# Joining three attention groups: merged at the end from three tiles, or one by one under a running maximum in one tile

## The chip, the cores and the metric

The kernel runs on one core of a Trainium2 chip. The time is the device time of one execution in microseconds (us). Three runs of the kernel before gave 960.3, 961.85 and 962.55 us, a median of 961.85. The core's engines are named as in the profile: PE (TensorE, matrix products), DVE (VectorE), ACT (ScalarE), POOL (GpSimd) and SP (SyncE, which here only issues transfers). ACT and POOL issue some transfers too. An engine takes its instructions in the order of the program; what one engine needs from another it waits for.

## The reference

One layer of a decoder trunk over 512 tokens of width 1024, in f32: a norm, one wide projection, two token mixers (retention and dilated attention), gates, an output projection, an MLP and a gated embedding. The change touches the attention alone. It has three groups of four heads (window and dilation 128 and 1, 512 and 4, 2048 and 16). Each group gives an output and a log-denominator, and the groups are joined by a softmax over these:

```
for g, (window, dilation) in enumerate(ATT_PATTERNS):
    o_g, lse_g = dilated_window_attention(aq[:, :, g], ak[:, :, g], av[:, :, g], window, dilation)
    ...
wts = jax.nn.softmax(jnp.stack(lses, axis=0), axis=0)
o = jnp.einsum('gbsh,gbshd->bshd', wts.astype(dt), jnp.stack(outs, axis=0))
att_branch = o.reshape(B, S, ATT_W) @ w_att_out
```

With m the maximum of a row of scores and l the sum of its exponentials, a group's weight is exp(m − M) · l over the sum of the same for all groups, M being the largest m.

## The kernel before, in words

**Products.** A product in f32 precision is made of three rounded ones (`mm3`, L257 to L262): each operand is split into a high and a low part. For weights this is `split_unit` (L234): a unit of 128x1024 arrives as `raw`, ACT writes `whi` (L248), DVE writes `wlo` = raw − whi (L249). PE runs through units six products of 128x512 at a time (`whi`, `wlo`, `whi` against the activations). Four `whi` and four `wlo` tiles exist, and units are split two ahead of their use. Some units are sums of weight blocks: POOL's queue adds a second block into `raw` by an accumulating transfer after the split (L226), or DVE adds two raw tiles (L224).

**Small jobs between products.** The attention's own steps are not written in line. `later(lag, fn, key)` (L111) puts a job into a queue with a due time; `tick` (L120), called after every few products, runs up to two due jobs at every second tick; `force(key)` (L130) runs jobs from the front of the queue until that one is done. So lags set where between the big products a transposition, a softmax or an evacuation stands in each engine's order. Behind that, a scheduler may still exchange neighbours on an engine.

**Attention.** For each group, `att_proj` makes q and k; `scores` (L732) runs four blocks r of 128 queries: four heads of scores into one bank `sc`, `softmax` (L657: DVE adds the mask, takes the maximum m, negates it as `nb`; ACT makes four exponentials `se` with their sums l), a transposition on PE into `pe`, its copy `pT`, and `weigh_values` (L768): values times `pT` into a bank `po`, copied into the group's tile `oT` of 128x4x512. Each of the three groups has its own `oT`. m and l of a group stand in `st`; those of group 0 are brought to the strided order of the others by way of DRAM (`to_strided`).

**Merge.** `merge` (L807) runs after the scores of group 2. DVE and ACT make the three groups' weights (16 columns each), PE transposes them in one bank `pc` (L845), ACT copies them out and its queue stores them in DRAM (`c_dram`, L848), and twelve loads of 256 KB on ACT's queue (L855) spread one row each over all partitions into tiles `cb`. For each head and group DVE multiplies a quarter of `oT` by its `cb` (L861) and adds it to group 0's (L863): twelve multiplications and eight additions of 128x512, four loads ahead of the multiplications. They fall into the time in which PE runs the projections `ret_proj` (its `rz`, `ro` and `kd` are on ACT and DVE, L955 and L570 to L575) and the first of the products of seven (`us`) for retention's values. `merged_split` (L878) splits the joined output much later, for the product with w_att_out.

Of the kernel before, what the change touches and what calls it, by code (L numbers as in the profile page):

```python
# [80 lines left out]
class Block:  # L81
# [575 lines left out]
    def softmax(self, sc, w, nh, mask, m, l):  # L657

        nc = self.nc
        s, e = self.tmp("sm"), self.tmp("se")  # L660
        sv = s[:, : nh * w].rearrange("p (h e) -> p h e", h=nh)
        nc.vector.tensor_tensor(sv, sc[:, : nh * w].rearrange("p (h e) -> p h e", h=nh),
                                mask.unsqueeze(1).to_broadcast([P, nh, w]), op=ALU.add)
        nc.vector.tensor_reduce(m, sv, axis=AX.X, op=ALU.max)
        nb = self.small(nh, "nb")
        nc.vector.tensor_scalar(nb, m, -SCALE, None, op0=ALU.mult)
        for h in range(nh):
            c = slice(h * w, (h + 1) * w)
            nc.scalar.activation(e[:, c], s[:, c], AF.Exp, bias=nb[:, h : h + 1], scale=SCALE,
                                 accum_out=l[:, h : h + 1])  # L670
        return e
# [9 lines left out]
    def attention(self):  # L681

        nc = self.nc
        with self.tc.manual_schedule(engines={nc.scalar.engine, nc.vector.engine}):
            qk = self.att_proj(0, 0), self.att_proj(0, 1)
        nc.sync.dma_start(self.mask, self.a["c_mask"])
        self.left = self.token_factors_seven()
        v0 = self.v_proj()
        self.gain_rows(1, NG)
        self.rot_rows(1)  # L690
        stats = [self.scores(0, *qk, v0, 2)]
        qk = [self.att_proj(1, 0)]
        self.later(4, lambda: stats.__setitem__(0, self.to_strided(stats[0])))
        qk.append(self.att_proj(1, 1))
        pT = self.big("pT")
        stats.append(self.scores(1, *qk, None, held=pT))
        v1, v2 = self.values_seven()
        values = self.weigh_values(1, v1, pT)
        for r in range(NT):
            self.force(("pT", 1, r))  # L700
            self.later(6, lambda r=r: values(r), ("att", 1, r))
        qk = self.att_proj(2, 0), self.att_proj(2, 1)
        self.spare = True
        stats.append(self.scores(2, *qk, v2))
        return stats
# [26 lines left out]
    def scores(self, g, qT, kT, v, lag=14, held=None):  # L732
# [3 lines left out]
        pTs = [[] for _ in range(NT)]  # L736

        def block(r):
# [4 lines left out]
            if not wide:  # L743
# [3 lines left out]
                es.append(self.softmax(sc, P, H, self.mask[:, 128 * (g + 1) : 128 * (g + 2)], m, l))  # L747
# [8 lines left out]
            for e in es:  # L756
                out = None if held is None else held[:, r]
                self.later(8, lambda e=e: pTs[r].append(self.transpose4(e, out)), ("pT", g, r))
            if v is not None:
                self.later(15, lambda: values(r), ("att", g, r))  # L760
# [7 lines left out]
    def weigh_values(self, g, v, pTs):  # L768

        nc = self.nc  # L770
        out = self.oT.setdefault(g, [])

        def values(r):
            if not out:
                out.append(self.big("oT"))
            oT = out[0]
# [13 lines left out]
            if g > 0:  # L790
                self.evac(oT[:, :, r * P : (r + 1) * P], pv)
            else:
                ov = oT.rearrange("p h (q a l) -> p h q a l", q=DIL, a=NT)
                self.evac(ov[:, :, :, r], pv.rearrange("p h (l q) -> p h q l", q=DIL))
# [12 lines left out]
    def merge(self, stats):  # L807
        nc = self.nc
        for r in range(NT):
            self.force(("sc", NG - 1, r))  # L810
        t3 = lambda s: self.sm.tile([P, NT, H], F32, tag="sm16", name=self.nm(s))
        M, den = t3("M"), None
        ms = [st[:, :, 0] for st in stats]
        ls = [st[:, :, 1] for st in stats]
        nc.vector.tensor_tensor(M, ms[0], ms[1], op=ALU.max)
        M2 = t3("M")
        nc.vector.tensor_tensor(M2, M, ms[2], op=ALU.max)
        es = []
        for g in range(NG):
            d, e, w = t3("d"), t3("e"), t3("w")  # L820
            nc.vector.tensor_tensor(d, ms[g], M2, op=ALU.subtract)
            nc.scalar.activation(e, d, AF.Exp, scale=SCALE)
            nc.vector.tensor_tensor(w, e, ls[g], op=ALU.mult)
            es.append(e)
            if den is None:
                den = w
            else:
                n = t3("n")
                nc.vector.tensor_tensor(n, den, w, op=ALU.add)
                den = n  # L830
        inv = t3("inv")
        nc.vector.reciprocal(inv, den)
        cs = []
        for g in range(NG):
            c = t3("c")
            nc.vector.tensor_tensor(c, es[g], inv, op=ALU.mult)
            cs.append(c)
        wide = self.const.tile([P, NG * H * NT], F32, name="cw")
        for g in range(NG):
            nc.vector.tensor_copy(wide[:, g * H * NT : (g + 1) * H * NT].rearrange("p (h r) -> p r h", h=H), cs[g])  # L840
        cd = self.dram.tile([NG * H, S], F32, name="c_dram", tag="c_dram")

        def turn():
            ps = self.bank("pc")
            nc.tensor.transpose(ps[: NG * H * NT, :P], wide, self.ident)  # L845
            turned = self.const.tile([P, P], F32, name="ct")[: NG * H * NT]
            nc.scalar.activation(turned, ps[: NG * H * NT, :P], AF.Copy)
            nc.scalar.dma_start(cd.rearrange("a (r l) -> (a r) l", r=DIL), turned)  # L848

        self.later(1, turn)  # L850
        spread = {}

        def load(h, g):
            c = spread[h, g] = self.tmp("cb")
            nc.scalar.dma_start(c, cd[g * H + h : g * H + h + 1].to_broadcast([P, S]))  # L855

        def weigh(h, g):
            if h == 0:
                self.force(("att", g, NT - 1))
            o, c, n = self.oT[g][0][:, h], spread.pop((h, g)), self.oT[0][0][:, h]  # L860
            nc.vector.tensor_tensor(o, o, c, op=ALU.mult)  # L861
            if g:
                nc.vector.tensor_tensor(n, n, o, op=ALU.add)  # L863

        items = [(h, g) for pair in ((0, 1), (2,)) for h in range(H) for g in pair]
        for i, (h, g) in enumerate(items):
            if i == 0:
                for p in items[:4]:
                    self.later(4, lambda p=p: load(*p))

            def step(i=i, h=h, g=g):
                if i + 4 < len(items):
                    load(*items[i + 4])
                weigh(h, g)
            self.later(7 + i, step, ("O", h, g))


    def merged_split(self, O):  # L878
# [5 lines left out]
        def split(h):  # L884
            self.force(("O", h, 2))
# [240 lines left out]
    def mix(self, A):  # L1126
# [14 lines left out]
        O = self.merged_split(self.oT[0][0])  # L1141
# [4 lines left out]
        for h in range(H):  # L1146
            self.force(("O", h, 2))
# [304 lines left out]
    def run(self):  # L1452
# [3 lines left out]
        self.oT = {}  # L1456
        stats = self.attention()
        self.later(21, lambda: self.merge(stats))
# [31 lines left out]
```

## Time and profile before

| what | value |
|---|---|
| median of three runs | 961.85 us |
| the profiled execution: its own time | 959.34 us |
| its span, first to last instruction | 957.6 us |
| busy: PE, DVE, ACT, POOL | 948.6, 730.6, 539.7, 148.5 us |
| transfers | 159.70 MB, mean 167 GB/s |

The profile is that of one execution. A row of a timeline gives the start and the length of one instruction (or of a run of alike ones, x4), then engine, line, operation, what is written and read, and in square brackets how long the engine sat idle before it and what ended that. A matmul row is 0.39 us long but the next starts 0.23 us after it, since products overlap: starts are to be compared, not lengths. The names of tiles lack their numbers there. "ACTq", "SPq" and POOL's transfer rows are issues of transfers.

### The profile page before, as it was taken

Reading aid. Unit: us, or ns where it says so; the run is one execution under the profiler, and the core shown is the slowest. Engines: PE = TensorE matmul, PEld = TensorE weight load, DVE = VectorE, ACT = ScalarE, POOL = GpSimd, SP = SyncE. Lnnn points to the kernel's source line nnn. Section 1 sums busy time; section 2 is a strip of 40 time slices with the busy share of each in tenths; the row PEclk is TensorE's granted clock in tenths of the full one; section 3 lists DMA queues with packets and bytes.
Section 4 is the critical chain, followed back from the end, with each engine's and each line's share of the span. In section 5 each row is a group of like instructions: output and inputs, shape, how many; then the busy total and the mean of one; then the engine's idle time right before and its main releaser. Section 6 shows DMA issues by size and latency. Waiting matters only on the chain.

```text
span 957.6 us, 14335 instructions
## 1 busy us (share of the span) xinstructions
PE 948.6 (99%) x5380; PEld 831.0 (87%) x5380; DVE 730.6 (76%) x1019; ACT 539.7 (56%) x1027; POOL 148.5 (16%) x132
## 2 busy tenths in 40 slices
PE   9999999999998999999999999999999999999998
PEld 7888888888887888999988888988998998998887
DVE  7878977578866948486937879799499579769953
ACT  6556456434464656477714445883484476467651
POOL 0310231022001111223012211211312202112100
PEclk9999999999999999999999999999999999999999
DMA  9851227434247564869748676968959868876911
GB/s 336 279 175 46 90 66 168 160 117 143 89 111 173 155 134 134 150 189 208 237 122 239 150 180 202 215 146 224 193 150 203 196 188 152 226 173 157 289 49 56
DMA packets 89605, 159.70 MB, mean 167 GB/s; under 512 B 7184, under 2 KB 19136, under 8 KB 89536
## 3 DMA queue, kind: packets, MB, share of 16 engines
q1 hardware_dynamic: 65840, 113.64, 35.8%
q0 software_dynamic: 21760, 41.95, 26.8%
q10 hardware_dynamic: 1936, 3.20, 1.1%
q8 instruction: 42, 0.69, 0.3%
q14 instruction: 27, 0.22, 0.1%
HBM read 150.33 MB, written 6.33 MB: 164 GB/s over the span
## 4 chain that ended last, share of the span: by engine, by line
PE 97%; DVE 2%; DMA 1%; issue 0%; ACT 0%; DVEq 0%
PE pg L260 27%; PE pg L261 27%; PE pg L262 27%; PE pa L262 3%; PE pa L260 3%; PE pa L261 3%; PE po L787 1%; PE ph L585 1%; PE sc L746 1%; DMA cb<-c_dram 1%; PE ry L1054 1%; PE pe L676 1%; PE kv L1041 1%; PE sc L752 1%; PE ry L1056 1%; DVE wlo L249 0%
## 5 line engine op out<-in xcount | busy, mean ns | idle before, releaser
L248 ACT ACTIVATE whi<-raw 128x1024 fp32r<-128x1024 f32 (+1 forms) x251 | 259.7, 1039 | 211.2 <-PE pg L262 85.5
L249 DVE TENSOR_TENSOR wlo<-raw,whi 128x1024 fp32r<-128x1024 f32 (+1 forms) x252 | 299.3, 1198 | 96.4 <-ACT whi L248 95.5
L260 PE MATMUL pg<-whi,hh 128*128 128x512 f32 x296 | 118.1, 400 | 0.0
L262 PE MATMUL pg<-whi,hl 128*128 128x512 f32 x296 | 115.6, 390 | 0.0
L261 PE MATMUL pg<-wlo,hh 128*128 128x512 f32 x296 | 115.3, 389 | 0.0
L260 PE MATMUL pg<-f,whi 128*128 128x256 f32 x384 | 108.7, 283 | 0.3 <-DVE r L1296 0.3
L261 PE MATMUL pg<-f,whi 128*128 128x256 f32 x384 | 108.7, 283 | 0.0
L262 PE MATMUL pg<-f,wlo 128*128 128x256 f32 x384 | 108.7, 283 | 0.0
L260 PE MATMUL pg<-whi,f 128*128 128x512 f32 x192 | 75.2, 392 | 0.0
L261 PE MATMUL pg<-wlo,f 128*128 128x512 f32 x192 | 74.8, 389 | 0.0
L262 PE MATMUL pg<-whi,f 128*128 128x512 f32 x192 | 74.7, 389 | 0.0
L260 PEld LDWEIGHTS pg<-f,whi 128*128 128x128 f32 x384 | 73.7, 192 | 0.7 <-ACT r L1298 0.5
L261 PEld LDWEIGHTS pg<-f,whi 128*128 128x128 f32 x384 | 73.7, 192 | 0.2
L262 PEld LDWEIGHTS pg<-f,wlo 128*128 128x128 f32 x384 | 73.7, 192 | 0.0
L262 PEld LDWEIGHTS pg<-whi,hl 128*128 128x128 f32 x296 | 55.6, 188 | 11.9
L261 PEld LDWEIGHTS pg<-wlo,hh 128*128 128x128 f32 x296 | 55.7, 188 | 10.8
L260 PEld LDWEIGHTS pg<-whi,hh 128*128 128x128 f32 x296 | 55.6, 188 | 10.9 <-ACT whi L248 0.3
L226 POOL DMA_DIRECT2D raw<-in_w_in x24 | 29.3, 1219 | 167.4 <-DVE wlo L249 152.5
L640 POOL TENSOR_TENSOR r<-v,mhalf 128x4 f32<-128x4 f32 x24 | 30.1, 1258 | 147.7 <-DVE v L639 142.0
L226 POOL DMA_DIRECT2D raw<-in_w_down x24 | 29.1, 1216 | 139.9 <-DVE wlo L249 108.8
L226 POOL DMA_DIRECT2D raw<-in_w_up x24 | 29.0, 1210 | 134.8 <-DVE wlo L249 124.4
L224 DVE TENSOR_TENSOR raw<-raw,raw 128x1024 f32<-128x1024 f32 x32 | 38.9, 1219 | 5.3 <-issue 2.9
(276 smaller groups left out, 2257.1 us busy)
## 6 DMA issues: line engine op xcount, KB each, us to landing
raw<-in_w_in SPq DMA_DIRECT2D x72, 512.0 KB, 3.8
raw<-in_w_up SPq DMA_DIRECT2D x32, 512.0 KB, 4.6
raw<-in_w_down SPq DMA_DIRECT2D x32, 512.0 KB, 4.5
raw<-in_w_in POOLq DMA_DIRECT2D x24, 512.0 KB, 6.8
raw<-in_w_up POOLq DMA_DIRECT2D x24, 512.0 KB, 7.3
raw<-in_w_down POOLq DMA_DIRECT2D x24, 512.0 KB, 6.5
x<-in_x SPq DMA_DIRECT2D x8, 512.0 KB, 8.3
raw<-in_w_ret_out SPq DMA_DIRECT2D x8, 512.0 KB, 4.1
```

Source lines behind the costliest of these rows:

```text
L224: self.nc.vector.tensor_tensor(total, total, part, op=ALU.add)
L226: self.nc.gpsimd.dma_start(raw, self.chained[i].rearrange("(k p) n -> p k n", p=P), accum_op=ALU.add)
L248: self.pin(nc.scalar.activation(R(hi[:, i]), raw[:, i], AF.Copy))
L249: nc.vector.tensor_tensor(R(lo[:, i]), raw[:, i], hi[:, i], op=ALU.subtract)
L260: t.matmul(ps, sh, mh, start=first, stop=False, skip_group_check=more)
L261: t.matmul(ps, sh, ml, start=False, stop=False, skip_group_check=more)
L262: t.matmul(ps, sl, mh, start=False, stop=last, skip_group_check=more)
L585: self.nc.tensor.transpose(ps[:, t * P : (t + 1) * P], rots[t][:, h * HD : (h + 1) * HD], self.ident)
L640: nc.gpsimd.tensor_tensor(r, v, self.mhalf[:, :H], op=ALU.pow)
L676: self.nc.tensor.transpose(ps[:, k * P : (k + 1) * P], e[:, k * P : (k + 1) * P], self.ident)
L746: nc.tensor.matmul(sc[:, h * P : (h + 1) * P], qT[:, h, rs], kT[:, h, rs], start=True, stop=True)
L752: nc.tensor.matmul(sc[:, h * 256 : (h + 1) * 256], qT[:, 2 * hp + h, rs], kT[:, 2 * hp + h, (r - 1) * P : (r + 1) * P], start=True, stop=True)
```

## The change

The three groups are joined one after another. Group 1's softmax takes, for each block, the larger of its own maximum and that of group 0 (`past`), group 2's that of the two before. When the scores of group 1 are done, `rescale(1, ...)` makes f = exp(m past − m new) for 16 columns, adds the sums up (l = l new + f · l past), and spreads f over the partitions by way of DRAM as `merge` did; four multiplications scale what group 0 has left in the one tile `oT`. Group 1's weighed values are then added from their bank `po` to that tile instead of being copied to a tile of their own. After the scores of group 2 the same is done once more, and here 1/l is multiplied into f, and into the 16 exponentials' tiles of group 2 (ACT, 128x128 each) before they are transposed. `merge` is gone. Group 2's transpositions are due three ticks later, its values too, and each `force`s its `rescale` first.

```diff
@@ softmax @@
-    def softmax(self, sc, w, nh, mask, m, l):
+    def softmax(self, sc, w, nh, mask, m, l, past=None):
...
         nc.vector.tensor_reduce(m, sv, axis=AX.X, op=ALU.max)
+        if past is not None:
+            nc.vector.tensor_tensor(m, m, past, op=ALU.max)
         nb = self.small(nh, "nb")
@@ attention @@
-        stats = [self.scores(0, *qk, v0, 2)]
+        first = self.scores(0, *qk, None, v0, 2)
         qk = [self.att_proj(1, 0)]
-        self.later(4, lambda: stats.__setitem__(0, self.to_strided(stats[0])))
+        strided = self.to_strided(first)
         qk.append(self.att_proj(1, 1))
         pT = self.big("pT")
-        stats.append(self.scores(1, *qk, None, held=pT))
+        past = self.scores(1, *qk, strided, held=pT)
+        self.later(22, lambda: self.rescale(1, strided, past), ("past", 1))
...
-            self.later(6, lambda r=r: values(r), ("att", 1, r))
+            self.later(8, lambda r=r: values(r), ("att", 1, r))
         qk = self.att_proj(2, 0), self.att_proj(2, 1)
         self.spare = True
-        stats.append(self.scores(2, *qk, v2))
-        return stats
+        last = self.scores(2, *qk, past, v2)
+        self.later(21, lambda: self.rescale(2, past, last), ("past", 2))
@@ scores @@
-                self.later(8, lambda e=e: pTs[r].append(self.transpose4(e, out)), ("pT", g, r))
+                self.later(8 if g < 2 else 11, lambda e=e: turn(e, r, out), ("pT", g, r))
             if v is not None:
-                self.later(15, lambda: values(r), ("att", g, r))
+                self.later(15 if g < 2 else 18, lambda: values(r), ("att", g, r))
+
+        def turn(e, r, out):
+            if g == 2:
+                self.force(("past", 2))
+            pTs[r].append(self.transpose4(e, out))
@@ weigh_values @@
         def values(r):
-            if not out:
-                out.append(self.big("oT"))
-            oT = out[0]
+            if g:
+                self.force(("scaled", g))
+            if not self.oT:
+                self.oT.append(self.big("oT"))
+            oT = self.oT[0]
...
             if g > 0:
-                self.evac(oT[:, :, r * P : (r + 1) * P], pv)
+                rs = oT[:, :, r * P : (r + 1) * P]
+                nc.vector.tensor_tensor(rs, rs, pv, op=ALU.add)
@@ merge, replaced by rescale @@
-    def merge(self, stats):
...
+    def rescale(self, g, past, st):
+
         nc = self.nc
         for r in range(NT):
-            self.force(("sc", NG - 1, r))
+            self.force(("sc", g, r))
         t3 = lambda s: self.sm.tile([P, NT, H], F32, tag="sm16", name=self.nm(s))
...
+        f, l = t3("f"), st[:, :, 1]
+        nc.vector.tensor_tensor(f, past[:, :, 0], st[:, :, 0], op=ALU.subtract)
+        nc.scalar.activation(f, f, AF.Exp, scale=SCALE)
+        w = t3("w")
+        nc.vector.tensor_tensor(w, f, past[:, :, 1], op=ALU.mult)
+        nc.vector.tensor_tensor(l, l, w, op=ALU.add)
+        if g == NG - 1:
+            inv = t3("inv")
+            nc.vector.reciprocal(inv, l)
+            nc.vector.tensor_tensor(f, f, inv, op=ALU.mult)
+            for r in range(NT):
+                e = self.es[g, r]
+                for h in range(H):
+                    c = slice(h * P, (h + 1) * P)
+                    nc.scalar.activation(e[:, c], e[:, c], AF.Copy, scale=inv[:, r, h : h + 1])
+        wide = self.const.tile([P, H * NT], F32, name=f"wide{g}")
+        nc.vector.tensor_copy(wide.rearrange("p (h r) -> p r h", h=H), f)
+        d = self.dram.tile([H, S], F32, name=f"f_dram{g}", tag=f"f_dram{g}")
+        spread = []
 
         def turn():
             ps = self.bank("pc")
-            nc.tensor.transpose(ps[: NG * H * NT, :P], wide, self.ident)
...
+            nc.tensor.transpose(ps[: H * NT, :P], wide, self.ident)
+            turned = self.const.tile([P, P], F32, name=f"turned{g}")[: H * NT]
+            nc.scalar.activation(turned, ps[: H * NT, :P], AF.Copy)
+            nc.scalar.dma_start(d.rearrange("a (r l) -> (a r) l", r=DIL), turned)
+
+        def load():
+            spread.append(self.big("fb"))
+            for h in range(H):
+                nc.scalar.dma_start(spread[0][:, h], d[h : h + 1].to_broadcast([P, S]))
+
+        def scale():
+            for h in range(H):
+                o = self.oT[0][:, h]
+                nc.vector.tensor_tensor(o, o, spread[0][:, h], op=ALU.mult)
 
         self.later(1, turn)
...
-            self.later(7 + i, step, ("O", h, g))
+        self.later(4, load)
+        self.later(12, scale, ("scaled", g))
@@ run @@
-        self.oT = {}
-        stats = self.attention()
-        self.later(21, lambda: self.merge(stats))
+        self.oT = []
+        self.attention()
```

`merged_split` and `mix` now wait for group 2's last values (`("att", 2, NT - 1)`) instead of the merge's steps.

Two places are shown in the program's order. The first is DVE before, in the stretch in which PE starts on the products of seven after group 2 (`wlo` are the low parts of weight units, `cb` the spread weights of one head and group, `oT` the groups' outputs):

```order
L249 TENSOR_TENSOR wlo_2858<-raw_2855,whi_2857 128x1024
L863 TENSOR_TENSOR oT_1188<-oT_1188,oT_1900 128x512
L249 TENSOR_TENSOR wlo_2887<-raw_2884,whi_2886 128x1024
L861 TENSOR_TENSOR oT_1188<-oT_1188,cb_2852 128x512
L861 TENSOR_TENSOR oT_1900<-oT_1900,cb_2877 128x512
L863 TENSOR_TENSOR oT_1188<-oT_1188,oT_1900 128x512
L861 TENSOR_TENSOR oT_1188<-oT_1188,cb_2881 128x512
L861 TENSOR_TENSOR oT_1900<-oT_1900,cb_2907 128x512
L249 TENSOR_TENSOR wlo_2917<-raw_2914,whi_2916 128x1024
```

Four multiplications, each with a `cb` of its own, stand ahead of the split `wlo_2917`. DVE in the change, a little earlier in the same stretch (`fb` is the spread f of all four heads, `ro`, `kd` and `rz` belong to `ret_proj`, `po` are the banks of group 2's values):

```order
L861 TENSOR_TENSOR oT_1192<-oT_1192,fb_2698 128x512 x4
L570 TENSOR_TENSOR ro_2757<-rz_2752,rotc_109 128x512
L573 TENSOR_TENSOR ro_2758<-rz_2752,rotc_109 128x4x64 x2
L249 TENSOR_TENSOR wlo_2804<-raw_2801,whi_2803 128x1024
L575 TENSOR_TENSOR kd_2686<-ro_2757,ro_2758 128x512
L570 TENSOR_TENSOR ro_2794<-rz_2789,rotc_109 128x512
L573 TENSOR_TENSOR ro_2795<-rz_2789,rotc_109 128x4x64 x2
L804 TENSOR_TENSOR oT_1192<-oT_1192,po_2828 128x4x128
L575 TENSOR_TENSOR kd_2686<-ro_2794,ro_2795 128x512
L804 TENSOR_TENSOR oT_1192<-oT_1192,po_2834 128x4x128
L804 TENSOR_TENSOR oT_1192<-oT_1192,po_2840 128x4x128
L804 TENSOR_TENSOR oT_1192<-oT_1192,po_2846 128x4x128
```

The next rows there are four splits without anything between them: `wlo_2853`, `wlo_2874`, `wlo_2896` and `wlo_2919`, the last being the unit that `wlo_2917` was. All use of spread factors now stands ahead of them, in one piece.

The second place is ACT after the exponentials of group 2. Before, from the fourth of these copies on:

```order
L955 ACTIVATE rz_2714<-pg_2558,dec 128x128 x4
L847 ACTIVATE ct<-pc_2725 48x128
L848 DMA c_dram<-ct 48x128
L855 DMA cb_2730<-c_dram 128x512
L955 ACTIVATE rz_2744<-pg_2571,dec 128x128 x4
L248 ACTIVATE whi_2798<-raw_2796 128x1024
L855 DMA cb_2755<-c_dram 128x512
L855 DMA cb_2757<-c_dram 128x512
```

In the change, from the exponential of f on:

```order
L828 ACTIVATE f_2614<-f_2614 128x16
L840 ACTIVATE se_2505<-se_2505,inv_2620 128x128 x4
L840 ACTIVATE se_2521<-se_2521,inv_2620 128x128 x4
L840 ACTIVATE se_2562<-se_2562,inv_2620 128x128 x4
L840 ACTIVATE se_2578<-se_2578,inv_2620 128x128 x4
L850 ACTIVATE turned_2657<-pc_2655 16x128
L248 ACTIVATE whi_2662<-raw_2660 128x1024
L851 DMA f_dram_2641<-turned_2657 16x128
L248 ACTIVATE whi_2669<-raw_2666 128x1024
L945 ACTIVATE rz_2687<-pg_2543,dec 128x128 x4
L945 ACTIVATE rz_2715<-pg_2588,dec 128x128 x4
L856 DMA fb_2698<-f_dram_2641 128x512 x4
```

Sixteen scalings stand ahead of the two splits `whi`, and the four spread loads are issued together, ahead of the copies of the transposed exponentials.

More of the change, by code (lines that the diff above doesn't have):

```diff
@@ L730, in values_seven, with scores @@
         return v
-    def scores(self, g, qT, kT, v, lag=14, held=None):
+    def scores(self, g, qT, kT, past, v=None, lag=14, held=None):
         nc = self.nc
@@ L736, in scores @@
         pTs = [[] for _ in range(NT)]
+        self.es = {}
         def block(r):
@@ L746, in block @@
                     nc.tensor.matmul(sc[:, h * P : (h + 1) * P], qT[:, h, rs], kT[:, h, rs], start=True, stop=True)
-                es.append(self.softmax(sc, P, H, self.mask[:, 128 * (g + 1) : 128 * (g + 2)], m, l))
+                es.append(self.softmax(sc, P, H, self.mask[:, 128 * (g + 1) : 128 * (g + 2)], m, l,
+                                       None if past is None else past[:, r, 0]))
+                self.es[g, r] = es[0]
             else:
@@ L770, in weigh_values @@
         nc = self.nc
-        out = self.oT.setdefault(g, [])
         def values(r):
-            if not out:
-                out.append(self.big("oT"))
-            oT = out[0]
+            if g:
[3 more added lines that the diff above has]
+            oT = self.oT[0]
             po = self.bank("po")
@@ L805, in to_strided @@
         return out
-    def merge(self, stats):
+    def rescale(self, g, past, st):
         nc = self.nc
         for r in range(NT):
-            self.force(("sc", NG - 1, r))
+            self.force(("sc", g, r))
         t3 = lambda s: self.sm.tile([P, NT, H], F32, tag="sm16", name=self.nm(s))
[L812 to L841, printed above, removed]
@@ L843, in turn @@
+        wide = self.const.tile([P, H * NT], F32, name=f"wide{g}")
+        nc.vector.tensor_copy(wide.rearrange("p (h r) -> p r h", h=H), f)
+        d = self.dram.tile([H, S], F32, name=f"f_dram{g}", tag=f"f_dram{g}")
+        spread = []
         def turn():
             ps = self.bank("pc")
-            nc.tensor.transpose(ps[: NG * H * NT, :P], wide, self.ident)
-            turned = self.const.tile([P, P], F32, name="ct")[: NG * H * NT]
-            nc.scalar.activation(turned, ps[: NG * H * NT, :P], AF.Copy)
@@ L848, in turn @@
-            nc.scalar.dma_start(cd.rearrange("a (r l) -> (a r) l", r=DIL), turned)
-        self.later(1, turn)
[L851 to L874, printed above, removed]
-            self.later(7 + i, step, ("O", h, g))
+            nc.tensor.transpose(ps[: H * NT, :P], wide, self.ident)
@@ L884, in split @@
         def split(h):
-            self.force(("O", h, 2))
+            self.force(("att", 2, NT - 1))
             av = O[:, h].rearrange("p (r l) -> p r l", r=DIL)
@@ L1140, in mix @@
                 self.force(("A", h, n))
-        O = self.merged_split(self.oT[0][0])
+        O = self.merged_split(self.oT[0])
         G = [self.big("Ga") for _ in range(2)]
@@ L1146, in mix @@
         for h in range(H):
-            self.force(("O", h, 2))
+            self.force(("att", 2, NT - 1))
             self.force(("split", h))
```

## Prediction

> **What bounds the kernel now.** I read the page first, then what PE waits for, then PE's timeline around the one long wait, then what DVE and ACT do there.
>
> ```profile
> PE 97%; DVE 2%; DMA 1%; issue 0%; ACT 0%; DVEq 0%
> PE pg L261 <- DVE wlo L249: 2.6, 1, 2.6
> ```
>
> The chain that ended last is PE for 97% of the span. So work that the change takes from DVE, ACT or the transfers is worth nothing in itself; it counts only where PE waits for it. The longest of PE's waits, 2.6 us and only once, is for the low part of a weight unit.
>
> ```profile
> 298.05 0.39 PE L260 MATMUL pg<-whi,us 128*128 128x512 f32 x1
> ...
> 300.76 0.39 PE L260 MATMUL pg<-whi,us 128*128 128x512 f32 x1
> 303.73 0.80 PE L261 MATMUL pg<-wlo,us 128*128 128x512 f32 x1 [2.58 <-DVE wlo L249]
> 304.33 0.63 PE L262 MATMUL pg<-whi,us 128*128 128x512 f32 x1
> 304.75 0.63 PE L260 MATMUL pg<-whi,us 128*128 128x512 f32 x1
> ...
> 306.99 0.39 PE L260 MATMUL pg<-whi,us 128*128 128x512 f32 x1
> 304.00:309.00 5.00, 5.00 (x17) 4.02 (x18) 5.00 (x7) 2.67 (x4) 1.22 (x1) 0.74 0.63 90
> ```
>
> Undisturbed, twelve matmuls take 300.76 − 298.05 = 2.71 us, 0.226 us each. From 300.76 to 306.99 there are nine steps, worth 2.03 us, and they took 6.23: **4.2 us are lost here**. 2.7 of them are the wait itself, 1.5 the matmuls behind it, which start 0.42 us apart until about 306.5; the last row (from a table of stretches, the granted clock third from the end) shows the clock at 0.74 there.
>
> ```profile
> 294.23 0.33 ACTq L855 DMA_DIRECT2D cb<-c_dram  x1
> ...
> 298.48 1.05 ACT L248 ACTIVATE whi<-raw 128x1024 fp32r<-128x1024 f32 x1
> 301.85 0.69 DVE L861 TENSOR_TENSOR oT<-oT,cb 128x512 f32<-128x512 f32 x1 [2.60 <-DMA cb<-c_dram]
> DMA to landing us min/median/max: 3.0/4.8/7.6
> ```
>
> The high part was ready at 299.5. The low part came just before PE's 303.73, because ahead of it on DVE stood a multiplication with a `cb` that was issued at 294.23 and landed 7.6 us later, the slowest of the twelve.
>
> **What goes.** The change's order has no multiplication between these splits any more: `wlo_2853` to `wlo_2919` follow each other, and nothing on DVE there waits for a spread load. The whole loss goes, if nothing else is late: −4.2 us. What is late next is the question below; between the splits it is only ACT's `whi`, ready early.
>
> **What is added on PE.** Two transpositions of 16 columns for one of 48. The row of the old one, with no wait beside it:
>
> ```profile
> 275.27 0.27 PE L845 MATMUL pc<-ident,cw 128*48 128x128 f32 x1
> ```
>
> One more costs between nothing (hidden in its neighbours, as matmuls overlap) and 0.27 us; I take 0.1. Everything else on PE is the same work in another place.
>
> **First junction, group 1 (about 181 to 211 us).** New on DVE are four multiplications and four additions of 0.6 us in place of two copies, 3.6 us more, and on ACT's queue a store and four loads.
>
> ```profile
> 190.16 0.69 DVE L160 COPY oT<-po 128x512 f32<-128x512 f32 x1 [6.10 <-PE po L787]
> 199.48 0.69 DVE L570 TENSOR_TENSOR ro<-pg,C 128x512 f32<-128x512 f32 x1 [2.98 <-ACT j L616]
> 210.41 0.68 DVE L570 TENSOR_TENSOR ro<-pg,C 128x512 f32<-128x512 f32 x1
> 211.01 0.74 DVE L573 TENSOR_TENSOR ro<-pg,S 128x256 f32<-128x256 f32 x2
> 181.75 1.05 ACT L248 ACTIVATE whi<-raw 128x1024 fp32r<-128x1024 f32 x1
> 192.42 1.06 ACT L248 ACTIVATE whi<-raw 128x1024 fp32r<-128x1024 f32 x1 [0.78 <-PE pg L262]
> 206.26 0.39 PE L260 MATMUL pg<-whi,hh 128*128 128x512 f32 x1
> 214.43 0.39 PE L260 MATMUL pg<-whi,hh 128*128 128x512 f32 x1
> c_dram<-ct ACTq DMA_DIRECT2D x1, 24.0 KB, 1.4
> ```
>
> I cost it at nothing, and the cover is DVE's idle time ahead of two of these rows alone, 6.1 + 3.0 = 9.1 us. The store goes out behind the split of 181.75, at about 183, lands 1.4 us later, and the loads, 0.33 us apart, are out by 185.9 and landed by 190.7 (median) or 193.5 (slowest); then come the last multiplication, three additions and two splits (4 × 0.6 + 2 × 1.14 = 4.7 us), which ends before DVE's next `ro` was due at 199.48. The last addition stands among the `ro`, where DVE has no idle time: the bank read at 211.01 to 211.7 is written again by PE at 214.43, so 0.6 of 2.7 us go. In the program's semaphores SP's last value store and the next weight loads wait for these loads; the unit split at 192.42 is first used at 206.26, 13.8 us later, and its two splits take 2.3 of these. ACT stands still for about 3 us where it idled before.
>
> **Second junction, group 2 (258 to 293 us): where a new wait could arise.** ACT makes sixteen scalings ahead of the splits, PE's transpositions are due three ticks later, and all four `fb` multiplications stand on DVE ahead of `wlo_2853`.
>
> ```profile
> 264.75 0.39 ACT L669 ACTIVATE se<-sm,nb 128x128 f32<-128x128 f32 x1
> 265.13 0.20 ACT L822 ACTIVATE e<-d 128x16 f32<-128x16 f32 x1
> 268.18 1.06 ACT L248 ACTIVATE whi<-raw 128x1024 fp32r<-128x1024 f32 x1 [0.30 <-PE pg L262]
> 269.14 1.07 ACT L156 ACTIVATE pT<-pe 128x512 f32<-128x512 f32 x2
> 271.83 1.14 ACT L955 ACTIVATE rz<-pg,dec 128x128 f32<-128x128 f32 x4 [1.62 <-PE pg L262]
> 272.84 0.62 ACT L156 ACTIVATE pT<-pe 128x512 f32<-128x512 f32 x1
> 266.72 0.17 DVE L823 TENSOR_TENSOR w<-e,st 128x16 f32<-128x16 f32 x1 [0.34 <-ACT e L822]
> 266.93 0.17 DVE L829 TENSOR_TENSOR n<-n,w 128x16 f32<-128x16 f32 x1
> 279.79 0.69 DVE L570 TENSOR_TENSOR ro<-rz,rotc 128x512 f32<-128x512 f32 x1 [1.06 <-ACT rz L955]
> 280.39 0.76 DVE L573 TENSOR_TENSOR ro<-rz,rotc 128x256 f32<-128x256 f32 x2
> 281.06 1.22 DVE L249 TENSOR_TENSOR wlo<-raw,whi 128x1024 fp32r<-128x1024 f32 x1
> 282.20 0.69 DVE L575 TENSOR_TENSOR kd<-ro,ro 128x512 f32<-128x512 f32 x1
> 282.80 0.68 DVE L861 TENSOR_TENSOR oT<-oT,cb 128x512 f32<-128x512 f32 x1
> 267.98 1.04 PE L676 MATMUL pe<-ident,se 128*128 128x128 f32 x8
> 280.85 1.95 PE L787 MATMUL po<-pT,v 128*128 128x128 f32 x16
> 292.83 0.39 PE L261 MATMUL pg<-wlo,us 128*128 128x512 f32 x1
> ```
>
> - Small DVE steps that need each other start 0.21 us apart. Four new maxima delay the last exponentials by 0.8 us, from 265.1 to 265.9. Exponential of f and five small steps bring 1/l at 266.9 and `wide` at 267.2. PE transposes it at 268.1, where the first of the old transpositions stood at 267.98 (+ 0.1): 0.9 us to spare, the smallest margin on PE.
> - The sixteen scalings: no such row exists. A copy with a scale out of a bank takes 0.25 us (four `rz` in 272.84 − 271.83), an exponential with a sum 0.38 (265.13 − 264.75); so 4.0 to 6.2 us. I take 4.0, the row of the same operation: they end at 270.9. The Trainium skill (ScalarE: Activation LUTs, What ACT_TABLE_LOAD costs) gives a cost per instruction by which a copy of 128 columns with a scale from a tile would start 0.29 us after the last, 4.7 us in all and within these ends; the four `rz` rows at 0.25 disagree with it a little.
> - Copy 0.3, two splits of 0.96, two `rz` groups of 1.01: 275.2. The four loads go out from 275.0 to 276.4, and the last lands 4.8 us after that (median), **at 281.2**. Ends: 279.4 (3.0 us) and 286.2 (scalings 2.2 us slower, landing 7.6).
> - From the last landing DVE needs its multiplication (0.60), `ro` 1.27, split 1.14, `kd` 0.60, `ro` 1.27, addition 0.60, `kd` 0.60, three additions 1.80, and `wlo_2853` 1.22: 9.1 us (additions from a bank at the 0.60 between 210.41 and 211.01). PE wants that split where it wanted its fellow before, at 292.83, + 0.1. **So the last `fb` may land at 283.8 at the latest**; by the median there are 2.6 us to spare. The split ahead of it is wanted twelve matmuls (2.7 us) earlier and is ready 6.0 us earlier.
> - PE's values read the four copies `pT`, which ACT makes behind the loads: from 276.4, four copies of 0.54, an `rz` group and a split, done by 280.6. The values stood at 280.85 before and stand two units of six matmuls and a little later now, so this costs nothing. POOL's accumulating transfers start behind these splits; for the first unit that is some 6 us later than before, for a use that comes 10 us after the stretch shown here. Nothing either.
>
> **Sum.** 959.34 − 4.2 + 0.1 = 955.2 us for the profiled execution. The median of the runs shown is 2.5 us above that execution; I take the same difference from it: 961.85 − 4.1 = **957.75 us**.
>
> **The rivals.**
> - *A new wait takes the place of the old.* If the last `fb` lands between 283.8 and 286.4, PE waits for `wlo_2853` by as much, and with a wait as long as before loses 1.5 us more by its clock. At the end worked out above, 286.2: 2.4 + 1.5 = 3.9 us, 961.65. For it: loads issued together with others landed at 7.6 us. Against: only four go out, and the four rows of scaling alone do not get there. 15%, half of it with so short a wait that the kernel is still faster.
> - *Slower.* The four loads wait on ACT's queue for the store `f_dram`, and rows of ACT wait behind them.
>
> ```profile
> r_dram<-r SPq DMA_DIRECT2D x1, 2.0 KB, 7.9
> ```
>
> A small store took 7.9 us here once, against 1.4 for `c_dram`. Issued at 272.2 it would land at 280.1, the loads go out until 281.5, and with 7.6 us the last lands at 289.1: PE waits 5.3 us + 1.5 for the clock, 957.75 + 6.8 = 964.5. It decides from a landing at 288.3 on (4.5 + 1.5 = 6 us, 963.8). That store fell in the crowded start of the program; 10%, 7 of them slower.
> - *The change does not do what it says for time:* the wait hangs on one transfer's 7.6 us; if the timed runs don't have it, only the 0.1 us is left: 961.95. Against it, the timed runs are slower than the profiled one, not faster. 9%.
> - *The clock's loss is not the wait's.* The rows show the low clock right behind the wait and nowhere else near, so I count it in. If its 1.5 us had another cause and stayed, the gain would be 2.7 − 0.1: 959.25, still faster. 4%. The Trainium skill (TensorE: Matmul & The Clock Gate, The HAM clock gate) has the clock fall after an idle window of some 3.4 us, and asks for no gaps longer than that. By that rule the 2.6 us wait was too short and this rival holds; the trace's clock of 0.74 after it says that the wait sufficed.
>
> **How the numbers follow.** Forecast 62%, the rivals 15, 10, 9 and 4. A measurement here can tell about 0.2% from no change, 1.9 us. Faster by more (below 959.9): 62 + 8 + 4 = 74%; within: 7 + 3 + 9 = 19%; slower: 7%. The low end of the range is what comes out if the 2.5 us between the profiled execution and the median are more of the same wait: 957.75 − 2.5 = 955.3. The high end, 961.7, takes in the new wait. Left out are the last of the rivals' cases, 16%.
>
> **What would show it.** In the new profile PE has no wait for `wlo` around 301 and the clock stays at 1.00 through 309; DVE's waits for `fb` end by 283; sixteen scalings in 4.0 us; `pc` at 268 without a wait; no wait at 214. It is wrong if PE waits at 292.9 for `wlo`, or at 268 for `wide`, or at 184 to 214 for a bank.

## The result, and the profile after

Five executions of each kernel on one chip, taken in turn: **956.12 us** median for the change (954.65 to 956.71), 960.86 for the kernel before (959.39 to 962.55). The ratio is 0.9948, with a 95% interval from 0.9932 to 0.9964: 4.7 us faster, where 4.1 had been forecast. The profiled execution of the change took 954.65 us with a span of 952.9.

First the chain of the page and the list of PE's waits after (us in total, times, longest):

```profile
PE 93%; DVE 3%; DMA 2%; ACT 1%; issue 1%; SPq 0%; DVEq 0%
PE warm L436 <- DVE warm L432: 1.4, 1, 1.4
PE pg L260 <- DVE r L1286: 0.4, 1, 0.4
```

The wait for `wlo` is gone, and nothing that the change touches has taken its place: what is left are the start of the program and 0.4 us far behind. The chain has less PE than before (93% for 97), but none of its steps on other engines lies where the change works: they stand in the first 102 us, such as the two below, or behind 567 us.

```profile
76.70 2.28 DVE wlo L249 x2
79.00 4.74 DMA raw<-in_w_in
```

The table of stretches of the change at the place of the old wait (granted clock third from the end):

```profile
299.00:304.00 5.00, 5.00 (x26) 4.17 (x25) 3.75 (x4) 3.03 (x4) 0.00 (x0) 1.00 1.10 227
304.00:309.00 5.00, 5.00 (x30) 4.30 (x29) 2.46 (x3) 3.91 (x7) 0.00 (x0) 1.00 0.59 173
```

The clock is 1.00 where it was 0.74. Where the time went is read from PE's timeline, before and then after, at three matmuls: the last point ahead of the old wait, one some 30 us behind it, and the last of the program:

```profile
292.61 0.39 PE L260 MATMUL pg<-whi,us 128*128 128x512 f32 x1
336.21 0.58 PE L260 MATMUL pg<-whi,hh 128*128 128x512 f32 x1
952.81 0.28 PE L262 MATMUL pg<-whi,h3l 128*128 128x256 f32 x1
```

```profile
292.60 0.39 PE L260 MATMUL pg<-whi,us 128*128 128x512 f32 x1
331.82 0.58 PE L260 MATMUL pg<-whi,hh 128*128 128x512 f32 x1
948.42 0.28 PE L262 MATMUL pg<-whi,h3l 128*128 128x256 f32 x1
```

At 292.6, with all of the first junction and most of the second behind them, the two kernels stand level to 0.01 us. (The changed one had begun its products 0.24 us later, at 11.14 against 10.90, and had made that up.) The gain on PE lies in the next 40 us: 336.21 − 331.82 = 4.4 us, and at the last matmul it is still 952.81 − 948.42 = 4.4. Behind the last matmul the rest of the span is 4.5 us instead of 4.8; that 0.3 is no part of the change.

The second junction after, on ACT (DMA issues have the engine name ACTq) and then on DVE:

```profile
266.93 4.80 ACT L840 ACTIVATE se<-se,inv 128x128 f32<-128x128 f32 x16 [0.80 <-DVE inv L834]
271.63 0.25 ACT L850 ACTIVATE turned<-pc 16x128 f32<-16x128 f32 x1
271.91 0.33 ACTq L851 DMA_DIRECT2D f_dram<-turned  x1
273.69 1.09 ACT L945 ACTIVATE rz<-pg,dec 128x128 f32<-128x128 f32 x4
274.52 0.33 ACTq L856 DMA_DIRECT2D fb<-f_dram  x1
275.44 0.34 ACT L945 ACTIVATE rz<-pg,dec 128x128 f32<-128x128 f32 x1
275.86 0.44 ACTq L856 DMA_DIRECT2D fb<-f_dram  x1
```

```profile
279.69 0.69 DVE L861 TENSOR_TENSOR oT<-oT,fb 128x512 f32<-128x512 f32 x1 [0.47 <-DMA fb<-f_dram]
283.44 0.69 DVE L861 TENSOR_TENSOR oT<-oT,fb 128x512 f32<-128x512 f32 x1 [1.05 <-DMA fb<-f_dram]
291.32 4.62 DVE L249 TENSOR_TENSOR wlo<-raw,whi 128x1024 fp32r<-128x1024 f32 x4
```

The sixteen scalings take 4.7 us (266.93 to 271.63). The last `fb` lands at 283.4, 7.6 us after its issue. In the kernel before PE's matmul started 1.27 us after the start of the split that it waited for (303.73 and 302.46). By that the first of the four splits is ready at 291.32 + 1.27 = 292.59, and PE wants it at 292.83. So the junction holds, by 0.2 us.

### The profile page after: what moved, and what is told of

It is laid out like the page before. It is cut to its first block, busy times and chain, and to the rows that moved or that the text cites. A ratio compares the mean times of both kernels' runs of the same rounds, so it can differ in the third digit from the quotient of the medians.

```text
span 952.9 us, 14339 instructions
## 1 busy us (share of the span) xinstructions
PE 946.5 (99%) x5381; PEld 829.7 (87%) x5381; DVE 728.2 (76%) x1014; ACT 541.5 (57%) x1037; POOL 148.6 (16%) x132
## 3 DMA queue, kind: packets, MB, share of 16 engines
q0 software_dynamic: 21760, 41.95, 26.6%
## 4 chain that ended last, share of the span: by engine, by line
PE 93%; DVE 3%; DMA 2%; ACT 1%; issue 1%; SPq 0%; DVEq 0%
PE pg L260 26%; PE pg L261 26%; PE pg L262 26%; PE pa L261 3%; PE pa L260 3%; PE pa L262 3%; PE po L799 1%; PE ph L585 1%; DVE wlo L249 1%; DMA raw<-in_w_in 1%; DMA raw<-in_w_down 1%; PE sc L750 1%; PE ry L1044 1%; PE kv L1031 1%; PE ry L1046 1%
```

## The experiments

The question was whether the 4.2 us were the wait and the clock behind it, or came from the work that the change saves on DVE and in the transfers; and how much room the second junction has. Ratios are against executions of the kernel before on the same chip (its median is 960.8 to 961.2 there). All runs:

| run | median us | ratio, 95% interval |
|---|---|---|
| before, twelve spread loads early | 958.34 | 0.9965 (0.9952–0.9979) |
| before, four spread loads in all | 956.74 | 0.9955 (0.9943–0.9968) |
| before, no additions | 958.89 | 0.9972 (0.9960–0.9984) |
| before, half the bytes in each spread load | 958.77 | 0.9979 (0.9967–0.9991) |
| change, scalings behind the store | 955.79 | 0.9943 (0.9931–0.9956) |
| change, 8 more scalings | 955.76 | 0.9945 (0.9933–0.9958) |
| change, 12 more | 957.72 | 0.9956 (0.9943–0.9970) |
| change, 16 more | 963.33 | 1.0007 (0.9990–1.0023) |
| change, 24 more | 957.38 | 0.9953 (0.9940–0.9967) |
| change, 16 more, half the bytes in `fb` | 959.12 | 0.9981 (0.9970–0.9993) |

### The wait taken from the kernel before

```diff
-            c = spread[h, g] = self.tmp("cb")
-            nc.scalar.dma_start(c, cd[g * H + h : g * H + h + 1].to_broadcast([P, S]))
+            if g not in spread:
+                spread[g] = self.big("cb")
+            nc.scalar.dma_start(spread[g][:, h], cd[g * H + h : g * H + h + 1].to_broadcast([P, S]))
...
+        for p in items:
+            self.later(4, lambda p=p: load(*p))
...
-                for p in items[:4]:
-                    self.later(4, lambda p=p: load(*p))
...
-                if i + 4 < len(items):
-                    load(*items[i + 4])
```

> The kernel before with nothing but its spread loads changed: all twelve are queued early into three tiles that nobody else waits for, instead of one by one into the small buffers that earlier multiplications give back. Additions, multiplications and bytes stay. My theory (the gain is the removed wait at 301 us and the low clock behind it, 2.7 + 1.5 us): the loads land before DVE asks for them, PE's wait for wlo goes, and this kernel gains about the same without merging anything: 956.7 us, 0.9956 of the time before (to 958 if a rest of the wait stays). Rival, the gain comes from the work that the change takes from DVE and the transfers (eight additions, eight spread loads less one for one): nothing of that is taken here, so 960.9, 1.000.

```diff
-            nc.scalar.dma_start(c, cd[g * H + h : g * H + h + 1].to_broadcast([P, S]))
+            nc.scalar.dma_start(spread[0][:, h], cd[h : h + 1].to_broadcast([P, S]))
...
-            o, c, n = self.oT[g][0][:, h], spread.pop((h, g)), self.oT[0][0][:, h]
+            o, c, n = self.oT[g][0][:, h], spread[0][:, h], self.oT[0][0][:, h]
```

> The kernel before with four spread loads instead of twelve: groups 1 and 2 are weighed with the factors of group 0 (part of the computation left out: their own factors), so that no multiplication waits for a later load. DVE's twelve multiplications and eight additions stay. My theory: no wait for wlo at 301, clock 1.00 behind it, 956.7 us, 0.9956. Rival, DVE's work makes the gain: 960.9, 1.000. If b_early keeps the time of before and this one gains, the wait is still the cause but early loads do not cure it; if neither gains, my theory falls.

Four loads in all give 956.74 us, with DVE's twelve multiplications and eight additions untouched: the whole gain of the change within the intervals. So **the work saved on DVE is not what pays.** (This run leaves out eight loads, so by itself it cannot tell their bytes from the waits for them; the run with half the bytes, below, moves fewer and gains less.) Twelve early loads keep every byte and every operation, and still gain 2.9 us, which the rival (960.9) does not allow; but they miss the 956.7 of my own theory. The two of PE's waits in that run that lie in this stretch (its profile is of the slowest of the five executions):

```profile
PE pg L260 <- DVE G L1010: 1.5, 1, 1.5
PE pg L261 <- DVE wlo L249: 0.3, 1, 0.3
```

The timeline of DVE and PE there, and two stretches (DVE's busy time is the fourth entry):

```profile
298.45 0.69 DVE L862 TENSOR_TENSOR oT<-oT,cb 128x512 f32<-128x512 f32 x1 [1.66 <-DMA cb<-c_dram]
303.92 0.69 DVE L862 TENSOR_TENSOR oT<-oT,cb 128x512 f32<-128x512 f32 x1 [1.59 <-DMA cb<-c_dram]
321.70 0.47 PE L260 MATMUL pg<-whi,hh 128*128 128x512 f32 x1 [1.55 <-DVE G L1010]
```

```profile
309.00:314.00 5.00, 5.00 (x23) 4.00 (x22) 5.00 (x7) 2.48 (x3) 0.00 (x0) 1.00 0.62 205
319.00:324.00 5.00, 3.45 (x18) 2.68 (x17) 5.00 (x7) 1.70 (x3) 0.00 (x0) 1.00 0.57 177
```

The long wait for `wlo` is down to 0.3 us and the clock stays at 1.00. But DVE still stands still for spread loads at 298 and 304, works off what piled up behind them without a break, and with PE 4 us ahead of its old pace the next thing is late: `G`, for 1.5 us. Of 4.2 us, 4.2 − 1.5 − 0.3 = 2.4 would be left. How well that fits is seen from the time that PE takes between the first two matmuls shown above in each profile (336.21 − 292.61 in the kernel before):

| run | PE's time, us | less than before | medians say |
|---|---|---|---|
| before | 43.60 | | |
| change | 39.22 | 4.4 | 4.7 |
| four spread loads in all | 39.31 | 4.3 | 4.5 |
| change, scalings behind the store | 39.26 | 4.3 | 5.4 |
| twelve spread loads early | 41.95 | 1.7 | 2.9 |
| no additions | 42.04 | 1.6 | 2.1 |
| half the bytes in each spread load | 42.18 | 1.4 | 2.0 |

So in the profiled execution with early loads 1.7 us are gained here, against 2.9 in the medians; but it is the slowest of its five: its products had begun 2.0 us late (12.90 against 10.90), at a place that the edit does not touch. The two groups, 4.3 to 4.4 and 1.4 to 1.7, are clear all the same. This is the answer to "what is late next": in the change nothing is, and no spread load stands on DVE after 283.4; in the old order something is. That the stops at 298 and 304 make `G` late is read from the order of the rows; the run with four loads, which has DVE's whole work and not these stops, has no wait for `G`.

```diff
             nc.vector.tensor_tensor(o, o, c, op=ALU.mult)
-            if g:
-                nc.vector.tensor_tensor(n, n, o, op=ALU.add)
```

> The kernel before without the eight additions on DVE that join the groups (part of the computation left out: groups 1 and 2 are not added). The multiplications, the twelve spread loads and their buffers stay. My theory: the late spread load near 294 is issued by PE's and ACT's pace and not by the additions, so the wait for wlo at 301 stays, at 2 to 2.6 us, with its low clock: 960.0 to 961.2 us. Rival, DVE's work makes the gain: 4.8 us of it are gone, 956 to 957.

```profile
PE pg L261 <- DVE wlo L249: 1.8, 2, 1.3
```

958.89 us lies between the two expectations. The wait did not stay at 2 to 2.6, as I had expected, nor did it go: it fell to 1.8 in two pieces, of 0.5 and 1.3, and behind both the clock is 1.00. 0.8 us less wait and 1.5 without a low clock are 2.3; the medians say 2.1, PE's timeline 1.6. What DVE's additions cost thus shows as wait of PE.

### How much room the second junction has

```diff
+            junk = [self.tmp("junk"), self.tmp("junk")]
             for r in range(NT):
                 e = self.es[g, r]
                 for h in range(H):
                     c = slice(h * P, (h + 1) * P)
+                    if r < 2:
+                        nc.scalar.activation(junk[r % 2][:, c], e[:, c], AF.Copy, scale=inv[:, r, h : h + 1])
                     nc.scalar.activation(e[:, c], e[:, c], AF.Copy, scale=inv[:, r, h : h + 1])
```

With 12, 16 and 24 more scalings the condition reads `r < 3`, `r < 4`, or makes two for each of the last two blocks.

> The changed kernel with eight more scalings on ACT among the sixteen, written to tiles that nobody reads: everything behind them on ACT, the four fb loads too, comes 2.4 us later. My theory: the last fb lands at 285.8 instead of 283.4, the split wlo wanted at 292.83 is ready at 294.85, PE waits 2.0 us there; the clock behind a wait of that length costs between nothing and 1.5: 958.1 to 959.6 us. Rival, the second junction has room enough: 956.1, the time of the changed kernel, and no wait for wlo near 293.

> The changed kernel with twelve more scalings on ACT, written to tiles that nobody reads. In the run with eight more, the fb loads went out as soon as the store of f had landed, and the split wanted near 293 was ready 0.1 us too late. With twelve the store goes out 3.6 us later than in the changed kernel, at 275.5, lands 1.4 to 2.6 us after that, the last load is issued 1.3 us later and lands 6.5 to 7.6 us after its issue: 284.7 to 287.0; the split follows 9.0 us later. My theory: PE waits 0.7 to 3.0 us at 293, and if 2.5 or more, loses up to 1.5 by the clock behind it: 956.8 to 960.6 us. Rival, the junction has room by other work moving up: no wait, 956.1.

With eight more, 955.76 us: no loss, where I had expected 2 to 3.5. ACT and DVE in that run:

```profile
274.51 0.32 ACTq L854 DMA_DIRECT2D f_dram<-turned  x1
275.88 0.81 ACTq L859 DMA_DIRECT2D fb<-f_dram  x2
276.29 0.59 ACT L948 ACTIVATE rz<-pg,dec 128x128 f32<-128x128 f32 x2
277.22 0.44 ACTq L859 DMA_DIRECT2D fb<-f_dram  x1
283.40 1.41 DVE L864 TENSOR_TENSOR oT<-oT,fb 128x512 f32<-128x512 f32 x2 [0.38 <-DMA fb<-f_dram]
291.99 4.62 DVE L249 TENSOR_TENSOR wlo<-raw,whi 128x1024 fp32r<-128x1024 f32 x4
```

The store went out 2.6 us later (274.51 against 271.91) but landed sooner, the last load was issued only 1.4 us later, and the last multiplication began at 284.1, 0.6 later than in the change. The split is ready at 291.99 + 1.27 = 293.26, and there PE's matmul starts, 0.15 us later than it would have:

```profile
293.26 0.50 PE L261 MATMUL pg<-wlo,us 128*128 128x512 f32 x1
```

With twelve more the delay gets through:

```profile
294.68 0.50 PE L261 MATMUL pg<-wlo,us 128*128 128x512 f32 x1 [1.15 <-DVE wlo L249]
```

1.15 us of wait, no low clock behind it, 957.72 us: 1.6 above the change and inside what was expected. Between eight and twelve more scalings lies the point from which the new wait shows in the time.

> The same with sixteen more scalings: store at 276.7, last landing 285.9 to 288.2 or later. My theory: PE waits 1.9 to 4.2 us for the split near 293, with the clock behind it 1.5 more: 958.0 to 961.8 us, so most of the gain is gone although nothing but idle ACT time was filled. If the wait of the kernel before and not its length by chance costs the clock, the stretch behind the new wait shows a granted clock below 1.00 too. Rival, no wait: 956.1.

> The same with twenty-four more scalings, 7 us later in all. My theory: 4 to 6.5 us of wait and 1.5 by the clock, 961.5 to 964.5 us: slower than the kernel before, which is the point from which the slower rival of the prediction decides. Rival, no wait: 956.1.

Sixteen more cost all of the gain, 963.33 us, beyond what I had expected, though the ten executions spread widely, from 959.47 to 965.48; twenty-four cost 1.3 us, far below it. The wait and the stretches with sixteen:

```profile
PE pa L260 <- DVE oT L804: 5.2, 1, 5.2
```

```profile
299.00:304.00 5.00, 3.27 (x8) 2.60 (x9) 5.00 (x9) 0.00 (x0) 1.20 (x1) 0.68 0.57 95
304.00:309.00 5.00, 5.00 (x23) 4.06 (x22) 4.92 (x5) 1.93 (x2) 1.22 (x1) 0.98 0.59 91
```

5.2 us of wait, and (0.32 + 0.02) × 5 = 1.7 us by the clock: 6.9 of the 7.2 us that the medians are apart. That is the price that the prediction's slower rival named, though on another path: PE waits here for the first addition of group 2's values (`oT`, L804), whose bank it writes next (`po` and `pa` take their banks from one pool), and not for a split. Why twenty-four are cheaper, the loads tell. Sixteen, then twenty-four:

```profile
281.16 0.33 ACTq L859 DMA_DIRECT2D fb<-f_dram  x1
282.11 1.55 ACTq L859 DMA_DIRECT2D fb<-f_dram  x2
287.67 0.69 DVE L864 TENSOR_TENSOR oT<-oT,fb 128x512 f32<-128x512 f32 x1 [1.72 <-DMA fb<-f_dram]
289.06 3.73 PE L799 MATMUL po<-pT,v 128*128 128x128 f32 x32
293.96 0.69 DVE L864 TENSOR_TENSOR oT<-oT,fb 128x512 f32<-128x512 f32 x1 [1.56 <-DMA fb<-f_dram]
```

```profile
280.97 0.33 ACTq L859 DMA_DIRECT2D fb<-f_dram  x1
282.31 0.44 ACTq L859 DMA_DIRECT2D fb<-f_dram  x1
287.82 1.89 DVE L864 TENSOR_TENSOR oT<-oT,fb 128x512 f32<-128x512 f32 x3
290.02 0.69 DVE L864 TENSOR_TENSOR oT<-oT,fb 128x512 f32<-128x512 f32 x1 [0.31 <-DMA fb<-f_dram]
```

The order is planned anew for each of these kernels. In both, the loads stand behind two more splits on ACT and go out at nearly the same time, 281 to 283; and PE's values stand later, at 289 to 290 where the change has them at 284, so what needs the loads comes later too. Yet the last `fb` lands at 293.9 in one, 11.3 us after its issue at 282.65, and at 290.0 in the other, 7.7 us after. These 3.9 us, and the 1.1 us by which PE asks later with twenty-four, are the difference between a wait of 5.2 us and one of 0.2. The next pair asked whether the loads' own bytes make it:

```diff
-            nc.scalar.dma_start(c, cd[g * H + h : g * H + h + 1].to_broadcast([P, S]))
+            a = g * H + h
+            nc.scalar.dma_start(c[:, : S // 2], cd[a : a + 1, : S // 2].to_broadcast([P, S // 2]))
...
-            nc.vector.tensor_tensor(o, o, c, op=ALU.mult)
+            for k in range(2):
+                oh = o[:, k * S // 2 : (k + 1) * S // 2]
+                nc.vector.tensor_tensor(oh, oh, c[:, : S // 2], op=ALU.mult)
```

> The kernel before with half the bytes in each of its twelve spread loads: only the first 256 of 512 columns are loaded, and both halves of a head are weighed with them (part of the computation left out: the factors of the second half). Order, queue and number of loads stay; DVE makes two multiplications of 256 columns for each one of 512. If the spread loads land late because their bytes share the 16 DMA engines with the weight transfers, the load issued near 294 lands 3 to 5 us later instead of 7.6, the wait for wlo at 301 goes or stays under 1 us without the low clock, and the time is 956.5 to 958. If the landing is set by the queue or its place, not by bytes: the wait of 2.6 us and 960.9 stay.

The same edit on the four `fb` loads of the run with sixteen more scalings:

> The run with sixteen more scalings again, with half the bytes in each of the four fb loads of group 2 (part of the computation left out: the factors of the second half of the columns). There the four landed 6.2 to 10.5 us after their issue, between 284 and 292 us the DMA engines were busy for the whole time, and PE waited 5.2 us at 300 (963.33 us). If bytes that share the DMA engines are the cause, the last fb lands by 289, PE's wait falls below 1.5 us, the clock stays at 1.00, and the time is 956.5 to 958.5. If the late issue alone is the cause, it stays at 961 to 963.

The landings of the spread loads, by their tile: in the kernel before, with half the bytes, with sixteen more scalings, and with both.

```profile
DMA to landing us min/median/max: 3.0/4.8/7.6
```

```profile
DMA to landing us min/median/max: 2.9/4.4/7.3
```

```profile
DMA to landing us min/median/max: 3.3/5.7/11.3
```

```profile
DMA to landing us min/median/max: 3.3/5.4/7.9
```

In the kernel before, half the bytes change the landing by 0.1 to 0.4 us, not by the 3 us that my theory asked for. The wait at 301 went all the same, but for a reason that the expectation had shut out: the order on DVE did not stay. Its rows in that run:

```profile
300.17 1.22 DVE L249 TENSOR_TENSOR wlo<-raw,whi 128x1024 fp32r<-128x1024 f32 x1
302.17 1.10 DVE L864 TENSOR_TENSOR oT<-oT,cb 128x256 f32<-128x256 f32 x3 [0.78 <-DMA cb<-c_dram]
```

In the kernel before eight multiplications stood ahead of this split (the eighth at 301.85, the split at 302.46). Here only fourteen halves, seven multiplications, do. The eighth load landed at 302.17, no earlier than before, but the split no longer stood behind it, and PE did not wait there. So this run confirms what made the old wait, and it is not a test of the bytes. As with the early loads a wait of 1.5 us for `G` came in its place (958.77).

With sixteen more scalings the slowest landing did fall, from 11.3 to 7.9, PE's wait from 5.2 to 1.8 us in the profiled execution, and the time from 963.33 to 959.12 (ten executions each), half a us above what I had expected. That the loads' own bytes do it is not shown: the order on DVE changed here too (the four additions of the values, at 295.36, now stand ahead of the splits, where two splits at 295.85 and 297.58 had stood ahead of them), and with twenty-four more scalings the slowest landing was 7.7 us with all of the bytes. What makes one load land after 3 us and another after 7 or 11 is left open; the weight transfers in the same stretch were not varied.

### More room

```diff
...
+        scalings(range(2))
...
             nc.scalar.dma_start(d.rearrange("a (r l) -> (a r) l", r=DIL), turned)
+            scalings(range(2, NT))
```

> The changed kernel with the last eight of the sixteen scalings moved behind the store of f, so that the store goes out 2.4 us earlier; the loads behind it follow the same rows on ACT as before and are issued at about the same time, so the last one lands where it did or a little earlier. My theory: PE waits for nothing of this any more, so more room gives nothing: 956.1 us (955.7 to 956.5). Rival, short waits for the splits behind the second junction still cost part of the time: 955 or below.

955.79 us, the time of the change. The first of the splits starts at 290.54 there, 0.8 us earlier. The 0.2 us by which it is early in the change are enough, and more room buys nothing.

## Why the prediction was right, point by point

- **The bound and the gain.** One wait of PE, 2.7 us, and 1.5 by the clock behind it: forecast −4.2, measured 4.4 on PE between the matmuls at 292.6 and 336.2. The run with four loads takes the same wait from the old kernel and gains 4.5 us (4.3 on PE there). Shown. The time itself is 1.6 us below the 957.75 forecast: 1.0 because the median of the kernel before is 960.86 over five executions and was 961.85 over the first three, 0.6 because the medians are 4.7 apart and not 4.1.
- **The transposition, +0.1.** It costs nothing that can be seen: PE is at 292.60 where it was at 292.61, although it had begun 0.24 us later.
- **First junction, nothing.** Right in the sum. The last `fb` multiplication of group 1 stood at 190.26 on DVE, and no wait of PE follows. ACT stood still for a weight load behind the `fb` loads, 9.34 us and not the 3 that I had given it. But ACT had been idle here before too (8.25 us, a copy, and 0.78 us), and the split starts at 192.37 where it started at 192.42, so it cost nothing.

```profile
192.37 1.06 ACT L248 ACTIVATE whi<-raw 128x1024 fp32r<-128x1024 f32 x1 [9.34 <-DMA raw<-in_w_in]
```

- **Second junction.** The steps up to 1/l were right to 0.1 us. Two sizes were wrong. The sixteen scalings took 4.7 us, not 4.0: I had taken the `rz` rows, which read a bank, and the estimate by the figures of the Trainium skill (ScalarE: Activation LUTs, What ACT_TABLE_LOAD costs), 0.29 us each, was right against them. And the last `fb` took 7.6 us to land, not the median of 4.8. A third error hid 1.3 of these 3.5 us: I had the loads wait for the two `rz` groups ahead of them on ACT, and they did not. Together 283.4 instead of 281.2, so 0.2 us of room instead of 2.6. The bounds (279.4 to 286.2) held it, the middle did not. The margin that kept the gain whole was therefore luck in its size.
- **New wait in place of the old.** It did not come, by 0.2 us. Its mechanism is real: 1.15 us with twelve more scalings.
- **Slower, by a late `f_dram`.** The store had landed when the first load went out, 2.6 us later, not 7.9. The price that the rival named, 5.3 us of wait and 1.5 of clock, is close to what sixteen more scalings showed, 5.2 and 1.7, but there it came from loads planned later and landing in up to 11.3 us, not from the store.
- **The change does nothing.** Falls: 4.7 us lie between the medians. Of the 45 executions of the kernel before beside the experiments, 37 show a mean clock of 0.995 to 0.998 and eight 0.999 or 1.000; all five of the change show 0.999 or 1.000. So the low clock, and with it presumably the wait, was in most of the runs; only the profiled one shows the wait itself. The eight are 0.9 us faster by their median than the others, not as fast as the change.
- **The clock's loss is not the wait's.** Falls: in the four kernels made from the old one in which the wait is gone or short, the clock behind 301 is 1.00, and a wait of 5.2 us made at another place brings 0.68. The rule that I had quoted from the Trainium skill (TensorE: Matmul & The Clock Gate, The HAM clock gate), a fall after some 3.4 us of idleness, would have let 2.58 us pass; the rows do not bear that out.
- **What the prediction did not see** is the wait for `G` that lies behind the one at 301. The two runs that left multiplications with spread loads between the splits, and took little more than the wait at 301 (early loads and half the bytes), gained 2.9 and 2.0 us.

## What to carry to other kernels

Before counting a wait as gained, ask what is late next at the faster pace: two cures of the same wait gave 2 to 3 us, and two others 4.5 to 4.7, by whether DVE still had to stop for transfers later on. Price a transfer on which a margin rests by its slowest landing, not its median. A row of the same operation that reads another memory is not the same row. And where a scheduler plans the order anew, compare the orders of both kernels before you put a difference down to the edit.

## What the runs showed of the hardware that was not expected

- **A PE wait of 2.58 us was followed by a lower clock.** Behind waits of 1.15, 1.31, 1.50, 1.55 and 1.83 us the stretches show a granted clock of 1.00; behind 2.58 us 0.74 over 5 us, behind 5.20 us 0.68. These are single traces, and the length alone does not seem to decide. In stretches of 0.5 us the clock was low from about 303.2 in the kernel before, some 2 us after PE had stopped; with the wait of 5.20 us it was still 1.00 at 300.5, 5 us after PE had stopped, and low only from about 300.8, when the wait was over. Both times it stayed low for 3.4 us, so the loss, 1.3 and 1.7 us by these rows, hardly grew with the wait. (In seven of the ten executions of the kernel with the wait of 1.83 us the mean clock was 0.997 or 0.998 all the same; how long they waited, no trace shows.)
- **DMA issues on ACT's queue went out before computations ahead of them had run.** In the order the four `fb` loads stand behind eight `rz` copies; with eight more scalings the first was issued at 275.88, before the first of them started at 276.29, as soon as the store had landed (1.37 us after its issue). The Trainium skill gives ScalarE's queue a depth of 8 (TensorE: Matmul & The Clock Gate, Architectural detail). Eight copies that have not begun fit that depth; no run here varies their number.
- **Landing times of like loads differ by 4 us at nearly the same time of issue**: the last of four landed at 290.0 and at 293.9, issued at 282.31 and 282.65.
